# An FFN up projection as seven block products a pair instead of eight, and its FFN in two halves with the activations in DRAM between them

## The chip, the cores and the metric

One NeuronCore of one Trainium2 chip runs the whole program in one launch. The metric is the device time of an execution in microseconds (us), smaller is better. Three timed runs of the kernel before gave 2637.28 to 2642.17 us, median 2638.38.

## The reference

A trunk of two layers over 1024 tokens of width 1024, all float32. Layer 0 mixes tokens with an mLSTM, layer 1 with differential attention. After each mixer comes a LayerNorm, and then the part that matters here, a gated FFN with a causal convolution of width 3 over the tokens:

```
u = x * (1 + sc2) + sh2
h = causal_dwconv(u @ w_up, conv_w, conv_b)     # w_up 1024 x 5632
a, g = split(h, 2)                              # 2816 columns each
y = (gelu(g) * a) @ w_down                      # w_down 2816 x 1024
x = layer_norm(alpha * x + (1 + g2) * y)
```

`sc2`, `sh2` and `g2` come from a conditioning vector through a matrix ("ada").

## The kernel before

Everything is laid out for 128 partitions. To keep float32 accuracy with TensorE's rounded format, each operand is split into a high part (rounded, by ScalarE's cast) and a low part (the rest, by a VectorE subtraction), and each product is three matmuls: high by high, high by low, low by high (`mm3`, L153). A matmul has 128 x 128 weights and 512 columns.

The 2816 hidden columns are 22 pairs: pair i is 128 columns of a and the 128 columns of g that gate them. For each part of a pair `up` (L687) takes one weight unit of 128 x 1024 (eight k tiles of 128), and multiplies it with the transposed normed tokens `uhi`, `ulo` in two halves of 512 tokens: per pair 2 parts x 2 token halves x 8 k tiles x 3 = 96 matmuls, into a PSUM accumulator `big` of two banks, of which there are two. ScalarE applies the last tap and the bias from PSUM (L698), VectorE the two other taps (L700), ScalarE the Gelu (L703), VectorE the product (L704), and both split the result into `ahi`, `alo` (L707, L708), which stay in SBUF.

`down` (L711) multiplies the activations of a group of pairs with their rows of w_down, for eight token tiles and two column halves, into one PSUM bank each (tags a and b, two banks each), and VectorE adds the bank to the residual `z` (L724, L726). `GROUPS` says how many pairs go into a group: 4, 4, 3, 3, 3, 5. After the first pair of a group, the down product of the group before is issued, so that up and down alternate through the FFN.

Weights come through `get` (L117): it issues the DMA of a unit up to four units ahead on SP's queue into one of three `raw` buffers, folds a row vector into it where there is one (`fold_down`, L1035: VectorE multiplies w_down by 1 + g2, L1037), and splits it (L113, L114). `plan` (L986) lists the units in the order of use.

Into an FFN leads `norm_to_u` (L343): per token tile statistics on VectorE and a power on GpSimd (L322), then the normed tile is transposed on TensorE in three groups of tiles (0 to 3, 4 and 5, 6 and 7), scaled and shifted out of PSUM (L300, L302) and split (L303, L304). The residual's own affine by rows (`finish_norm`, L371, L372) is handed out in steps, on VectorE, beside the first pairs. The ada vectors that layer 1 needs are summed on VectorE (L212, L214) between the groups of layer 0's FFN, the last one (for g2 of layer 1) at the entry to layer 1's FFN.

Instructions are traced in program order and put into the engines' queues by a list scheduler that takes, for each engine, what its own timing model holds to be ready, earlier traced first. Tiles of a pool with the same tag share its buffers, and one waits until another is free. `queued` (L132) holds TensorE's instructions in the order of tracing.

## Time and profile before

| | |
|---|---|
| median of three timed runs | 2638.38 us |
| the profiled execution | 2637.58 us |
| its span, first to last instruction | 2635.7 us |
| mean granted TensorE clock | 0.996 |
| busy TensorE, VectorE, ScalarE, GpSimd | 2577.2, 1612.1, 906.6, 56.0 us |
| DMA | 191.97 MB, mean 73 GB/s |

In the profile PE is TensorE's matmul side, PEld its weight loads, DVE VectorE, ACT ScalarE, POOL GpSimd, SP the engine that issues most DMAs. "idle <- X" is the time an engine sat idle before an instruction and what ended it. `out<-in` names the tiles; L126 is the line of `mm`, so matmuls are told apart by tiles: `big<-uhi,whi` is an up product (or a projection of the mLSTM), `bank<-whi,ahi` a down product. The granted clock is 1.00 at 2.4 GHz; the lower of its two levels is 1.2 GHz. Layer 0's FFN runs from about 582 to 1350 us, layer 1's from 1889 to the end.

### The profile page before, as it was taken

How to read it: one execution, taken by the hardware profiler on the slowest of the kernel's cores; microseconds unless marked ns; L12 is line 12 of the kernel's file. 1: busy time of each engine (PE TensorE's matmuls, PEld its weight loads, DVE VectorE, ACT ScalarE, POOL GpSimd, SP SyncE). 2: the span in 40 equal slices, each digit the busy share in tenths (PEclk: the TensorE clock that was granted, in tenths of full speed). 3: DMA queues.
4: the chain of work that ended last, by engine and by line, in shares of the span. 5: the costliest groups of instructions: out<-in, count | busy, mean ns of one | idle time of the engine just before them, and what ended most of it. 6: DMA issues, size and time to landing. Idle time of an engine off the chain costs nothing.

```text
span 2635.7 us, 30418 instructions
## 1 busy us (share of the span) xinstructions
PE 2577.2 (98%) x12380; PEld 2143.3 (81%) x12380; DVE 1612.1 (61%) x2407; ACT 906.6 (34%) x1465; POOL 56.0 (2%) x83
## 2 busy tenths in 40 slices
PE   7999999999999999999999999999999999999998
PEld 5887788877888888888788888878778888888887
DVE  7647546668646466465576777787784444544457
ACT  4423333244212122123246666674432222222120
POOL 0000000000000000000000000000000000000001
PEclk9999999999999999999999999999999999999999
DMA  6415312211313133131131101111221111111102
GB/s 264 144 33 175 96 40 65 85 60 50 103 56 104 56 118 114 48 112 35 56 132 35 35 27 35 35 53 49 102 88 40 56 41 60 52 41 56 48 32 80
DMA packets 59451, 191.97 MB, mean 73 GB/s; under 512 B 6640, under 2 KB 13104, under 8 KB 59312
## 3 DMA queue, kind: packets, MB, share of 16 engines
q1 hardware_dynamic: 56480, 184.30, 20.5%
q10 hardware_dynamic: 2832, 5.74, 0.7%
q8 instruction: 97, 1.59, 0.2%
q14 instruction: 42, 0.34, 0.0%
HBM read 180.04 MB, written 9.98 MB: 72 GB/s over the span
## 4 chain that ended last, share of the span: by engine, by line
PE 86%; DVE 8%; ACT 3%; DMA 1%; issue 1%; POOL 0%; DVEq 0%; ACTq 0%; SPq 0%; POOLq 0%
PE big L126 44%; PE bank L126 40%; PE bank L129 2%; DVE wlo L114 1%; DVE acc L214 1%; ACT whi L113 1%; DMA raw<-in_ada 1%; ACT p L867 1%; DVE qk L466 1%; DVE acc L255 1%; DVE ulo L304 1%; DMA wt<-mscr 0%; DVE col L857 0%; DVE kk L812 0%; DVE z L371 0%
## 5 line engine op out<-in xcount | busy, mean ns | idle before, releaser
L126 PE MATMUL big<-uhi,whi 128*128 128x512 f32 x1664 | 648.5, 391 | 4.2 <-ACT y L698 2.0
L126 PE MATMUL big<-ulo,whi 128*128 128x512 f32 x1664 | 649.7, 390 | 1.8 <-DVE ulo L304 1.6
L126 PE MATMUL big<-uhi,wlo 128*128 128x512 f32 x1664 | 648.1, 389 | 0.0
L113 ACT CAST whi<-raw 128x1024 fp32r<-128x1024 f32 x204 | 211.6, 1052 | 809.9 <-PE big L126 454.3
L114 DVE TENSOR_TENSOR wlo<-raw,whi 128x1024 fp32r<-128x1024 f32 x204 | 247.0, 1222 | 337.9 <-ACT whi L113 331.5
L126 PEld LDWEIGHTS big<-uhi,whi 128*128 128x128 f32 x1664 | 312.2, 188 | 70.5 <-ACT y L698 2.4
L126 PEld LDWEIGHTS big<-ulo,whi 128*128 128x128 f32 x1664 | 312.3, 188 | 68.6 <-DVE ulo L304 4.1
L126 PEld LDWEIGHTS big<-uhi,wlo 128*128 128x128 f32 x1664 | 312.4, 188 | 64.3 <-issue 0.2
L126 PE MATMUL bank<-whi,ahi 128*128 128x512 f32 x704 | 274.7, 390 | 0.0
L126 PE MATMUL bank<-wlo,ahi 128*128 128x512 f32 x704 | 274.7, 390 | 0.0
L126 PE MATMUL bank<-whi,alo 128*128 128x512 f32 x704 | 274.0, 390 | 0.0
L700 DVE SCALAR_TENSOR_TENSOR y<-big,pp,y 128x1023 f32<-128x1023 f32 (+1 forms) x176 | 225.0, 1278 | 2.6 <-ACT y L698 0.4
L726 DVE TENSOR_TENSOR z<-z,bank 128x512 f32<-128x512 f32 x160 | 109.5, 685 | 143.9 <-PE bank L126 143.5
L126 PE MATMUL bank<-whi,hot 128*128 128x512 f32 x512 | 175.1, 404 | 3.6 <-ACT hot L386 2.1
L126 PE MATMUL bank<-whi,uhi 128*128 128x256 f32 (+1 forms) x480 | 171.5, 358 | 2.2 <-ACT v L799 2.0
L126 PE MATMUL bank<-wlo,uhi 128*128 128x256 f32 (+1 forms) x480 | 160.7, 335 | 0.0
L126 PE MATMUL bank<-whi,ulo 128*128 128x256 f32 (+1 forms) x480 | 160.1, 336 | 0.0
L126 PEld LDWEIGHTS bank<-wlo,ahi 128*128 128x128 f32 x704 | 132.1, 188 | 29.8 <-issue 2.2
L126 PEld LDWEIGHTS bank<-whi,ahi 128*128 128x128 f32 x704 | 132.2, 188 | 28.6 <-ACT ahi L707 0.5
L126 PEld LDWEIGHTS bank<-whi,alo 128*128 128x128 f32 x704 | 132.1, 188 | 28.4 <-issue 1.1
L698 ACT ACTIVATE y<-big,pp 128x1024 f32<-128x1024 f32 x88 | 106.1, 1206 | 50.0 <-PE big L126 50.0
L126 PEld LDWEIGHTS bank<-whi,hot 128*128 128x128 f32 x512 | 96.1, 188 | 24.7 <-ACT hot L386 2.9
(226 smaller groups left out, 3512.1 us busy)
## 6 DMA issues: line engine op xcount, KB each, us to landing
raw<-in_up SPq DMA_DIRECT2D x88, 512.0 KB, 3.3
raw<-in_ada SPq DMA_DIRECT2D x80, 512.0 KB, 3.3
raw<-in_dn SPq DMA_DIRECT2D x44, 512.0 KB, 3.3
ada<-in_ada SPq DMA_DIRECT2D x16, 512.0 KB, 8.5
raw<-in_vo SPq DMA_DIRECT2D x16, 512.0 KB, 4.2
raw<-in_qk SPq DMA_DIRECT2D x16, 512.0 KB, 4.3
raw<-in_dqk SPq DMA_DIRECT2D x16, 512.0 KB, 3.3
xt<-in_xT SPq DMA_DIRECT2D x8, 512.0 KB, 9.6
```

The lines of the kernel that those rows point to most:

```text
L113: nc.scalar.copy(hi[:, :n], raw[:, :n])
L114: nc.vector.tensor_sub(lo[:, :n], raw[:, :n], hi[:, :n].bitcast(F32))
L126: self.last = self.nc.tensor.matmul(out, lhsT=lhsT, rhs=rhs, start=start, stop=stop, **kw).ins
L129: self.last = self.nc.tensor.transpose(out, in_, self.idn if idn is None else idn).ins
L214: nc.vector.scalar_tensor_tensor(acc, raw, self.cs[:, k:k + 1], acc, op0=ALU.mult, op1=ALU.add)
L255: last = nc.vector.scalar_tensor_tensor(acc, raw[:, i, :], c, acc, op0=ALU.mult, op1=ALU.add).ins
L304: nc.vector.tensor_sub(lo, tmp, hi.bitcast(F32))
L466: nc.vector.scalar_tensor_tensor(t[:, d:], ps[:, :S - d], wc(3 - d), t[:, d:], op0=ALU.mult, op1=ALU.add)
L698: nc.scalar.activation(y, ps, AF.Identity, bias=self.pp[:, base + 132 + ch:base + 132 + ch + 1], scale=wc(2))
L700: nc.vector.scalar_tensor_tensor(y[:, d:], ps[:, :S - d], wc(2 - d), y[:, d:], op0=ALU.mult, op1=ALU.add)
L726: nc.vector.tensor_add(z, z, ps)
L867: nc.scalar.activation(p[:, :nk], ps_[c][:, :nk], AF.Exp, bias=mx[:, c:c + 1], accum_out=sums[:, c, i:i + 1])
```

## The change

The up products of a pair form a 2 x 2 block product: the parts a and g by the two token halves, over two halves of the contraction (four k tiles each). Strassen's scheme (in Winograd's form) does it with seven block products instead of eight. It needs sums of weight blocks (`sums`, four additions of 128 x 512 on GpSimd per pair), sums of token blocks once at the entry (`ffn_entry`: T1 to T4, on VectorE and GpSimd), and sums of products (`p1` to `p7`, copies on ScalarE, additions on VectorE). One half comes out with its sign turned, so the convolution taps of g are negated at the start. The convolution now reads SBUF tiles `ca` and `cg` instead of PSUM. P3 and P4 of a pair are issued in the turn of the next one.

All 22 pairs go first. Their activations are stored in DRAM (`ascr`), and the down half loads them again and splits them beside the down weights (`prepare`); the fold of 1 + g2 goes to GpSimd. The groups are 3, 4, 4, 4, 4, 3. The normed residual is stored at the entry (`nscr`), loaded before the down half, and its affine is done there on GpSimd. The ada vectors are taken in single steps, in layer 0 all in the down half, in layer 1 in the up loop. The FFN's units leave `plan`, and its second weight pool is gone in layer 1.

The core of the diff:

```diff
-GROUPS = (4, 4, 3, 3, 3, 5)
+GROUPS = (3, 4, 4, 4, 4, 3)
...
+        nc.vector.tensor_scalar(taps, taps, -1.0, None, op0=ALU.mult)
...
+    def product(self, out, w, b, first):
+        (whi, wlo) = w
+        for j, (bhi, blo) in enumerate(b):
+            c = slice(j * P, (j + 1) * P)
+            self.mm3(out, whi[:, c], wlo[:, c], bhi, blo, first and j == 0, j == 3, skip_group_check=True)
+
+    def ffn_entry(self, zs, fp, ln, layer, early):
...
+                if t0 == 0:
+                    B["11" if k < 4 else "21"][k % 4] = parts(dst, self.up, "u", 24)
+            if t0 == 0:
+                early(B)
+        for j in range(4):
+            top, bot = u[j], u[4 + j]
+            nc.vector.tensor_sub(top[:, lo_], top[:, hi_], top[:, lo_])
+            nc.gpsimd.tensor_tensor(top[:, hi_], bot[:, hi_], top[:, hi_], op=ALU.subtract)
+            hi, lo = wide(top, self.up, "u", 24)
+            B["T1"][j], B["T3"][j] = (hi[:, lo_], lo[:, lo_]), (hi[:, hi_], lo[:, hi_])
+            B["22"][j] = parts(bot[:, hi_], self.up, "u", 24)
+            nc.vector.tensor_sub(bot[:, hi_], bot[:, hi_], top[:, lo_])
+            nc.gpsimd.tensor_tensor(bot[:, lo_], bot[:, hi_], bot[:, lo_], op=ALU.subtract)
+            hi, lo = wide(bot, *((self.up, "u", 24) if j < 2 else (fp, "f", 17)))
+            B["T4"][j], B["T2"][j] = (hi[:, lo_], lo[:, lo_]), (hi[:, hi_], lo[:, hi_])
...
+        def sums(i):
+            if i < NPAIR:
+                st1[i], st2[i] = ftile("st1"), ftile("st2")
+                add = lambda o, x, y: nc.gpsimd.tensor_tensor(o, x, y, op=ALU.add)
+                add(st1[i][:, lo_], rg[i][:, lo_], rg[i][:, hi_])
+                add(st1[i][:, hi_], st1[i][:, lo_], ra[i][:, lo_])
+                add(st2[i][:, lo_], ra[i][:, lo_], rg[i][:, lo_])
+                add(st2[i][:, hi_], ra[i][:, hi_], st1[i][:, hi_])
...
+        def p1(i):
+            pa[i] = self.bigbank()
+            with self.queued():
+                self.product(pa[i][:, lo_], cut(wx[i], lo_), B["11"], True)
+            cg[i] = ftile("cg")
+            nc.scalar.copy(cg[i][:, lo_], pa[i][:, lo_])
...
+        def p3(i):
+            with self.queued():
+                self.product(pc[i], w4[i], B["22"], False)
+            nc.vector.tensor_add(ca[i][:, hi_], ca[i][:, hi_], pc[i])
+            return conv(ca[i], i)
+
+        def p4(i, ya):
+            with self.queued():
+                self.product(pa[i][:, hi_], ww[i], B["T4"], False)
+            nc.vector.tensor_add(cg[i][:, lo_], cg[i][:, lo_], pa[i][:, hi_])
+            yg = conv(cg[i], NPAIR + i)
             nc.scalar.activation(yg, yg, AF.Gelu)
             nc.vector.tensor_mul(ya, ya, yg)
...
+            nc.sync.dma_start(out=self.ascr[i], in_=ya)
...
+        for i in range(NPAIR):
+            if i > 1:
+                p1(i)
+            prep_rest(i)
+            load(i + 2, 0)
+            sums(i + 1)
+            p5(i)
+            if i > 1:
+                p2(i)
+            if i:
+                prep_x(i + 1)
+            if i > 1:
+                next(beside_up, None)
+            load(i + 2, 1)
+            p6(i)
+            prep_y(i + 1)
+            if i:
+                ya = p3(i - 1)
+                p4(i - 1, ya)
+            if i == NPAIR - 1:
+                prepare_to(2)
+            p7(i)
+        for tt in range(NT):
+            zs[tt] = utile("z", F32)
+            nc.scalar.dma_start(out=zs[tt], in_=self.nscr[tt * P:(tt + 1) * P, :])
...
+        for tt in range(NT):
+            nc.gpsimd.tensor_tensor(zs[tt], zs[tt], rows[0], op=ALU.mult)
+            nc.gpsimd.tensor_tensor(zs[tt], zs[tt], rows[1], op=ALU.add)
```

## Rows read from the trace of the kernel before

**Rows 1.** The page: each engine's busy time, share of span, instructions.
```profile
PE 2577.2 (98%) x12380; PEld 2143.3 (81%) x12380; DVE 1612.1 (61%) x2407; ACT 906.6 (34%) x1465; POOL 56.0 (2%) x83
```

**Rows 2.** The page: the chain that ended last, by engine.
```profile
PE 86%; DVE 8%; ACT 3%; DMA 1%; issue 1%; POOL 0%; DVEq 0%; ACTq 0%; SPq 0%; POOLq 0%
```

**Rows 3.** Stretches: length, busy time (instructions) by engine, clock, DMA.
```profile
core 0: us, PE busy (x) PEld busy (x) DVE busy (x) ACT busy (x) POOL busy (x), PEclk, DMA share, GB/s
582.30:618.30 36.00, 31.51 (x162) 24.11 (x160) 35.77 (x55) 27.05 (x48) 1.42 (x1) 1.00 0.22 74
...
700.00:1310.00 610.00, 609.53 (x2678) 498.19 (x2677) 330.34 (x359) 138.00 (x130) 2.20 (x4) 1.00 0.23 77
...
1888.60:1931.50 42.90, 38.10 (x189) 29.14 (x188) 40.74 (x65) 29.76 (x50) 1.96 (x2) 1.00 0.50 172
...
2000.00:2565.00 565.00, 565.00 (x2494) 467.83 (x2493) 267.18 (x257) 130.53 (x123) 0.00 (x0) 1.00 0.14 48
```

**Rows 4.** Chain in time, layer 1: start, length, engine, tile, line, matmuls.
```profile
2062.30 87.04 PE big L126 x384
2149.34 43.52 PE bank L126 x192
...
2573.66 54.43 PE bank L126 x240
```

**Rows 5.** VectorE's groups by shape: busy us, mean ns, idle before.
```profile
L114 DVE TENSOR_TENSOR wlo<-raw,whi 128x1024 fp32r<-128x1024 f32 x204 | 247.0, 1222 | 337.9 <-ACT whi L113 331.5 <-PE bank L129 4.8 <-PE bank L126 0.4
L700 DVE SCALAR_TENSOR_TENSOR y<-big,pp,y 128x1022 f32<-128x1022 f32 x88 | 112.6, 1280 | 2.2
...
L726 DVE TENSOR_TENSOR z<-z,bank 128x512 f32<-128x512 f32 x160 | 109.5, 685 | 143.9 <-PE bank L126 143.5
L214 DVE SCALAR_TENSOR_TENSOR acc<-raw,cs,acc 128x1024 f32<-128x1024 f32 x70 | 89.5, 1279 | 15.9 <-DMA raw<-in_ada 15.6
...
L304 DVE TENSOR_TENSOR ulo<-utmp,uhi 128x512 fp32r<-128x512 f32 x24 | 16.3, 685 | 2.8 <-ACT uhi L303 2.8
...
L300 DVE TENSOR_SCALAR utmp<-bank,as,ab 128x256 f32<-128x256 f32 x16 | 8.0, 533 | 0.0
```

**Rows 6.** ScalarE's groups by shape, as above.
```profile
L113 ACT CAST whi<-raw 128x1024 fp32r<-128x1024 f32 x204 | 211.6, 1052 | 809.9 <-PE big L126 454.3 <-PE bank L126 283.1 <-DMA raw<-in_up 32.7
L698 ACT ACTIVATE y<-big,pp 128x1024 f32<-128x1024 f32 x88 | 106.1, 1206 | 50.0 <-PE big L126 50.0
L703 ACT ACTIVATE y<-y 128x1024 f32<-128x1024 f32 x44 | 46.7, 1062 | 125.0 <-DVE y L700 124.9
...
L386 ACT CAST hot<-bank 128x512 fp32r<-128x512 f32 x32 | 18.6, 587 | 40.2 <-PE bank L129 40.2
```

**Rows 7.** Timeline, GpSimd's power and VectorE beside it: start, length, instruction.
```profile
579.09 0.55 POOL L322 TENSOR_TENSOR col<-col,mhalf 128x1 f32<-128x1 f32 x1 [4.91 <-DVE col L321]
...
588.21 1.23 DVE L371 TENSOR_TENSOR z<-z,lng 128x1024 f32<-128x1024 f32 x1
588.42 1.42 POOL L322 TENSOR_TENSOR col<-col,mhalf 128x1 f32<-128x1 f32 x1 [8.79 <-DVE col L321]
589.35 0.68 DVE L304 TENSOR_TENSOR ulo<-utmp,uhi 128x512 fp32r<-128x512 f32 x1
...
1457.55 1.65 POOL L906 TENSOR_TENSOR col<-col,mhalf 128x8 f32<-128x8 f32 x1 [114.90 <-DVE col L905]
```

**Rows 8.** The page's DMA issues: queue, count, KB, median us to landing.
```profile
raw<-in_up SPq DMA_DIRECT2D x88, 512.0 KB, 3.3
```

**Rows 9.** Layer 1's norm: TensorE matmuls in time, and stretches (columns: rows 3).
```profile
1341.22 0.28 PE L126 MATMUL bank<-wlo,uhi 128*128 128x256 f32 x1
...
1352.36 0.41 PE L126 MATMUL bank<-wlo,uhi 128*128 128x256 f32 x1
...
1345.00:1350.00 5.00, 3.79 (x14) 2.11 (x14) 3.48 (x8) 3.96 (x10) 0.00 (x0) 0.61 0.00 0
1350.00:1360.00 10.00, 8.01 (x51) 8.02 (x52) 7.12 (x10) 2.14 (x8) 0.00 (x0) 0.68 0.46 177
```

**Rows 10.** Timeline, VectorE's last z additions, with the idle time before.
```profile
2621.31 0.69 DVE L726 TENSOR_TENSOR z<-z,bank 128x512 f32<-128x512 f32 x1 [1.10 <-PE bank L126]
...
2628.11 0.69 DVE L726 TENSOR_TENSOR z<-z,bank 128x512 f32<-128x512 f32 x1 [1.10 <-PE bank L126]
```

More of the change, by code (lines that the diff above doesn't have):

```diff
@@ L214, in ada_vector @@
                 nc.vector.scalar_tensor_tensor(acc, raw, self.cs[:, k:k + 1], acc, op0=ALU.mult, op1=ALU.add)
-        self.ada_late = (layer, n, acc)
+            if k == KT - 1:
+                self.ada_late = (layer, n, acc)
+            yield
+    def ada_vector(self, layer, n, pool):
+        for _ in self.ada_steps(layer, n, pool):
+            pass
     def finish_ada(self):
@@ new lines, in early @@
+        def early(b):
+            nonlocal B
+            B = b
+            p1(0)
+            p2(0)
+            load(1, 1)
+            prep_x(1)
+            p1(1)
+            p2(1)
+        B = None
+        load(0, 0)
+        load(0, 1)
+        load(1, 0)
+        sums(0)
+        prep_x(0)
+        self.ffn_entry(zs, fp, ln, layer, early)
+        prep_y(0)
+        groups, i = [], 0
+        for g in GROUPS:
+            groups.append(list(range(i, i + g)))
+            i += g
+        act, dn, held = {}, {}, {}
@@ new lines, in ffn, with fetch @@
+        homes = [(ftile,) * 4 + (utile,) * 8] + [(utile, ftile) * 8] * 4 + [(ftile,) * 8 + (wtile,) * 4]
+        work = []
+        for g, members in enumerate(groups):
+            slots = iter(homes[g])
+            for m in members:
+                for kind in range(2):
+                    work.append((g, m, kind, (next(slots), next(slots))))
+        def fetch(x):
+            if x < len(work) and x not in held:
+                g, m, kind, _ = work[x]
+                held[x] = self.raw()
+                nc.sync.dma_start(out=held[x], in_=(self.ascr[m], self.a["dn"][layer, m])[kind])
@@ new lines, in prepare, with prepare_to @@
+        def prepare(x):
+            g, m, kind, slots = work[x]
+            fetch(x)
+            fetch(x + 1)
+            raw = held.pop(x)
+            if kind:
+                nc.gpsimd.tensor_tensor(raw, raw, self.gb[(layer, 1)], op=ALU.mult)
+            hi, lo = (s(n, F32R) for s, n in zip(slots, ("dhi", "dlo")))
+            (act, dn)[kind][m] = hi, lo
+            nc.scalar.copy(hi, raw)
+            nc.vector.tensor_sub(lo, raw, hi.bitcast(F32))
+        done = 0
+        def prepare_to(n):
+            nonlocal done
+            while done < n:
+                prepare(done)
+                done += 1
@@ new lines, in ffn @@
+        for tt in range(NT):
+            zs[tt] = utile("z", F32)
+            nc.scalar.dma_start(out=zs[tt], in_=self.nscr[tt * P:(tt + 1) * P, :])
+        rows = self.ln_rows(self.wa, ln, "w", 8)
+        ya = p3(NPAIR - 1)
+        prepare_to(4)
+        p4(NPAIR - 1, ya)
+        prepare_to(2 * GROUPS[0])
+        for tt in range(NT):
+            nc.gpsimd.tensor_tensor(zs[tt], zs[tt], rows[0], op=ALU.mult)
+            nc.gpsimd.tensor_tensor(zs[tt], zs[tt], rows[1], op=ALU.add)
+        for g, members in enumerate(groups):
+            base = done
+            more = 2 * GROUPS[g + 1] if g + 1 < len(groups) else 0
+            late = after() if after and g + 1 == len(groups) else None
@@ L726, in down @@
                         nc.vector.tensor_add(z, z, ps)
+                    prepare_to(base + min(more, (more * (2 * tt + half + 1) + 13) // 14))
+                    if half:
+                        next(beside_down, None)
                     for _ in range(3):
-                        if after and after[0] <= tt - 1:
-                            after[0] = next(after[1], NT + 9)
-            if after:
-                for _ in after[1]:
-                    pass
-        pending, i, first = None, 0, True
-        for gi, g in enumerate(GROUPS):
-            members = list(range(i, i + g))
-            i += g
-            for n, m in enumerate(members):
-                up(m)
-                for _ in range(min(3, len(steps))):
-                    steps.pop(0)()
-                if n == 0 and pending is not None:
-                    down(pending, first)
-                    first = False
-            pending = members
-            self.finish_ada()
-            if gi < len(fillers):
-                fillers[gi]()
-        down(pending, first, after and after())
+                        if late and late[0] <= tt - 1:
+                            late[0] = next(late[1], NT + 9)
+            if late:
+                for _ in late[1]:
+                    pass
+            elif g + 2 == len(groups):
+                for _ in beside_down:
+                    pass
     def rel_bias(self):
```

198 lines of the change are left out of this document (120 added, 78 removed).

## The prediction

> **What bounds the kernel now.** I read the page's engine row first: TensorE is busy for 98% of the span [rows 1], and the chain that ended last is 86% TensorE and 8% VectorE [rows 2]. A busy share can hide short waits, so I looked at stretches: in the bodies of both FFNs (700 to 1310 us and 2000 to 2565 us) TensorE works 609.5 of 610 and 565.0 of 565 us at full clock, and VectorE 330 and 267 us [rows 3]. There the chain runs in pieces of 384 matmuls in 87.04 us and 192 in 43.52 us, both 0.2267 us a matmul [rows 4]. So the body is bound by the number of matmuls, and a matmul less is 0.2267 us less as long as the others keep up. The two entries to an FFN (582 to 618, 1889 to 1931 us) are different: VectorE is busy 35.8 of 36.0 us and 40.7 of 42.9 us, TensorE 31.5 and 38.1 us [rows 3]. They are bound by VectorE. The sum below is made against the profiled execution, 2637.6 us (span 2635.7 and 1.9 around it), 0.8 below the median of 2638.4.
>
> **What goes.** An up pair has eight block products of 12 matmuls (four k tiles by three terms), 96 x 0.2267 = 21.76 us; afterwards seven, 84 x 0.2267 = 19.04. Over 44 pairs that is 528 matmuls, **-119.7 us**. The down projection keeps its 1056 matmuls a layer.
>
> **The up loop.** Per pair VectorE gets three 512-wide subtractions for w3, w4, ww (0.685 each), one 1024-wide for x (1.222), one scalar_tensor_tensor for y (1.279), five 512-wide additions of products (0.685), four convolution steps (1.28), one product (1.22) [rows 5]: 14.3 us in 15 instructions. Back to back a next one starts 0.09 early (588.21 + 1.23 against 589.35, [rows 7]), so some 13.0 us. ScalarE gets five 512-wide copies (0.587), two 1024-wide (1.052), two biases (1.206) and the Gelu (1.062): 8.5 us [rows 6]. GpSimd gets four 512-wide additions, for which the trace has no row. From below, its shortest instruction is 0.55 us; from above, its power over eight elements took 1.65 against 0.55 for one, 0.16 us an element, which would make 80 us of 512 [rows 7]. That is another function; an addition is nearest to VectorE's row for the same shape, so I take GpSimd's fixed 0.55 and that 0.685, 1.23 us, 4.9 a pair. All three fit under 19.04 us: TensorE should stay the bound on average.
>
> The tight place is an order, not a sum. A pair's last product, P4, is issued one pair late, and the product block P1 of the pair after needs the accumulator that P4 leaves; only P7 (2.72 us) lies between. VectorE's addition that empties it stands behind the other half's convolution: after P3 ends, addition 0.69, ScalarE's bias 1.21, two steps 2.38, together 4.27, which is 1.55 after P4 ends; with its own 0.69 it is done at 2.24 of 2.72. Slack: 0.5 us. And GpSimd's four additions for the next pair fall there: their second operand lands about 3.3 us after its issue [rows 8], which waits for x to be split, some 12 us into the pair, so they start near 15.5 of 19, when those convolution steps begin. Do the engines disturb one another? GpSimd's one-element power takes 0.55 us, but 1.42 where it started 0.21 us into a VectorE operation on two SBUF tensors, and it ended when that had [rows 7]. So GpSimd waits for VectorE; whether VectorE waits for a long GpSimd operation no row shows. The Trainium skill, in "SBUF — State Buffer", section "SBUF: two separate sides", says that the two share one pair of ports and that the first to start holds it for its whole instruction, the other blocked; the 1.42 us row agrees with that for one side. By that rule two waits of up to 1.23 eat the 0.5 us and cost 2.0 us a pair, which is a rival below. I take 0.4 us a pair over some 42 pairs, **+17** (0 to +84).
>
> **The entries.** The change takes VectorE's z affine and, in layer 1, eight ada steps of 1.28 out of the entry, and the splitting of some weights. It adds, for each of four j, three 512-wide and two 1024-wide operations (3 x 0.685 + 2 x 1.22 = 4.5 us, 4.1 back to back [rows 5]), 16.4 in all, with eight GpSimd subtractions beside. VectorE's list then: two x splits 2.3, eight block splits 4.9, eight 256-wide affines 3.6 (0.53 each, less the overlap), last tile's addition and statistics 2.5, blocks 16.4, y 1.2: 31 us. Full rate can begin near 33 us after the last mixer matmul, where before it was 36 and 42.9. But before then TensorE had 96 matmuls done, and now 48 early ones and perhaps 10 of P5 and P6, the rest needing the last j: 38 x 0.2267 = 8.6 us behind. So +5.6 in layer 0 and -1.3 in layer 1. To that come the latencies of five engine changes in the last j, some 3 us each layer, and the clock: in the norm ahead of the attention, after waits and sparse transposes, the granted clock of two stretches was 0.61 and 0.68, between the 2.4 and the 1.2 GHz level, and 256-wide matmuls took 0.41 instead of 0.28 us [rows 9]; I take 2 us a layer. Together +14; with GpSimd's subtractions (8 x 1.23 = 9.8 a layer) in VectorE's way for 3 of that in each **+20** (+6 to +34).
>
> **The turn from up to down.** Before, the last pairs' activations were ready long before use, since up and down alternated. Now the down half begins 5.4 us (P3, P4) after the last P7. In that time VectorE has to end two pairs (about 10.5 us from these rows) and split operands of members 1 and 2 of the first group (four times 1.22 less the overlap, 4.5) and P7's sums (1.2): some 16 us. Four banks of PSUM let TensorE start members that are there, up to 5.4 us more. 16 - 10.8 leaves 5 to 6 us a layer. Then z: its affine, 16 VectorE passes a layer before, moves to GpSimd, with 22 folds of the down weights (on VectorE any two-tensor operation of 1024 takes 1.22 [rows 5]). At 0.55 + 1.22 = 1.77, sixteen passes and seven folds until the first group ends are 41 us, and from z's reload (its buffers come free with the last P2, 16 us before the down half, less 3.3 for the DMA [rows 8]) to the group's end (144 matmuls, 32.6 us) there are 46 us. It just fits; I add 3 us a layer. **+18** (+4 to +50). "GPSIMD Engine Reference", section "Elementwise — side-by-side cycle accounting", in the Trainium skill, gives 4497 ns for 2048 elements of such an addition; by an estimate from it a pass is 2.2 us and the 41 become 51, 5 us late a layer, no row here shows it.
>
> **The tails.** In layer 1's last group VectorE waits 1.10 us in each period of 6.80 [rows 10]: 5.7 us of work for a token tile that TensorE takes 6.80 for (five members, 54.43 us in all [rows 4]). With three members TensorE takes 4.08, VectorE still 5.7: the last group lasts 2 + 8 x 5.7 + 2 = 50 us where 32.6 + the old 7.6 us after the last matmul would be 40. **+9.** In layer 0 the norm of the next layer has the same group beside it; its VectorE work nearly equals TensorE's, **+4** (both 5 to 22 together).
>
> **At nothing:** 44 activation stores and reloads and the z rows each way, 63 MB in all. A pair's three transfers of 512 KB in 19 us are 83 GB/s; the body moved 77 GB/s at a DMA share of 0.23 [rows 3]. The store waits on SP for the pair's last product with the next loads behind it; these are wanted a pair later. If raw's three buffers fail to cover that, the wait is 3.3 us for some pairs. The ada vectors of layer 1 go into the down half (40 x 1.28 = 51 us of VectorE in 239), the sign of the gate taps is one small operation at the start, 0.5 us.
>
> Sum: -119.7 + 17 + 20 + 18 + 13 + 0.5 = -51; 2637.6 - 51 = **2586 us**, own range 2556 to 2615.
>
> **Rivals.**
> A. GpSimd and VectorE block each other, and P4's accumulator comes free late: 2.0 us x 42 = 84, entries at 34, turn at 38, tails 13: +49, 2687 us. From (119.7 - 52) / 42 = 1.6 us a pair it ends slower than before. For it: the 1.42 us row and the timing above. Against: VectorE kept its 0.68 us right beside GpSimd at 589.35 [rows 7], and if that addition goes ahead of the convolution steps, nothing is late.
> B. Nearly all is covered: up loop 0, entries +8, turn +6, tails +10: -96, 2542 us. For it: every engine's sum is under 19.04. Against: entries and tails are VectorE-bound already.
> C. The up loop holds, but z's passes and folds on GpSimd come late and the down half waits with full banks, 15 us a layer instead of 3: 2610 us.
>
> **Chances.** Forecast 0.52, A 0.18, B 0.17, C 0.13. A ends faster than before in a sixth of its part. Differences under 0.2% (5 us) can't be told here: faster 0.80, same 0.05, slower 0.15. Range 2542 to 2645: it takes in C and most of B, and A up to 1.7 us a pair.
>
> **What would show it.** Each steady pair: 84 matmuls in 19.0 to 19.8 us; over 20.6 is rival A, and the wait before P1 then names VectorE's addition. GpSimd's additions at 1.2 us, or longer where VectorE runs. After the last mixer matmul a TensorE gap of about 10 us at the entry, one of 5 to 9 at the turn, VectorE without waits in the last group. Wrong altogether if a steady matmul takes more than 0.227, or if the loop waits for a load.

## The result

The changed kernel takes 2778.23 us (median of 4 runs, 2776.4 to 2782.76) where the kernel before took 2640.2 beside it: 1.0526 times as long (95% interval 1.0508 to 1.0545), 5% slower. The forecast was 2586, in a range of 2542 to 2645: wrong in sign and size. The figures from here to the experiments are from a profiled execution with a span of 2776.6 us, 140.9 more than before. By stage (the first instruction of one to the first of the next) that is +6.3 in the mLSTM, +77.3 in layer 0's FFN (847.0 against 769.7), +0.6 in the attention and +56.7 in layer 1's FFN (803.8 against 747.1).

The page of the kernel after: engines, and the chain that ended last (answering to [rows 1, 2]).

```profile
PE 2523.6 (91%) x11852; PEld 2063.0 (74%) x11852; DVE 1931.9 (70%) x2692; ACT 1045.5 (38%) x1675; POOL 593.4 (21%) x351
...
PE 74%; DVE 10%; ACT 5%; POOL 4%; DMA 4%; issue 3%; DVEq 0%; POOLq 0%; ACTq 0%; SPq 0%
```

The 528 matmuls are gone (12380 to 11852), but TensorE fell from 98% busy to 91%. Its waits, summed over the execution (waiting tile and line, releaser: us, times, longest):

```profile
PE bank L126 <- ACT dhi L892: 54.6, 7, 13.4
PE big L126 <- ACT ca L802: 53.5, 39, 1.9
PE bank L126 <- DVE dlo L893: 26.0, 4, 12.4
PE bank L126 <- ACT uhi L711: 24.8, 6, 4.6
```

Three kinds of place: many short ones (ca: 39 of them, one in nearly every pair), a few long ones for a down operand (dhi, dlo: the turns), and the entries (uhi). Stretches of the kernel after (columns as in [rows 3]): layer 0's up loop, its turn, layer 1's entry:

```profile
640.00:1070.00 430.00, 398.76 (x1709) 318.83 (x1709) 328.48 (x310) 173.76 (x206) 147.68 (x85) 0.99 0.23 79
1077.00:1135.00 58.00, 19.26 (x65) 14.03 (x63) 35.52 (x18) 10.67 (x11) 53.34 (x19) 0.67 0.23 81
1967.00:2035.00 68.00, 45.11 (x190) 31.81 (x189) 50.33 (x65) 36.62 (x54) 21.54 (x15) 0.80 0.11 42
```

Before, TensorE was idle for 0.5 us of the 1175 us that [rows 3] shows of the two bodies. Now it idles 7% of the loop and two thirds of the turn, where GpSimd is busy 53 of 58 us. On top of these waits the granted clock of the turn is 0.67, between the two levels.

One pair of the up loop, in layer 0: GpSimd first, then VectorE, ScalarE and TensorE (start, length, instruction).

```profile
825.23 3.22 POOL L765 TENSOR_TENSOR st<-raw 128x512 f32<-128x512 f32 x2 [13.76 <-DMA raw<-in_up]
828.41 1.74 POOL L765 TENSOR_TENSOR st<-st,raw 128x512 f32<-128x512 f32 x1
830.22 2.15 POOL L765 TENSOR_TENSOR st<-raw,st 128x512 f32<-128x512 f32 x1
```

```profile
827.31 1.68 DVE L786 TENSOR_TENSOR w<-st,w 128x512 fp32r<-128x512 f32 x1
828.92 2.31 DVE L826 SCALAR_TENSOR_TENSOR y<-ca,pp,y 128x1023 f32<-128x1023 f32 x1
831.15 0.67 DVE L838 TENSOR_TENSOR cg<-cg,big 128x512 f32<-128x512 f32 x1
831.75 1.70 DVE L826 SCALAR_TENSOR_TENSOR y<-ca,pp,y 128x1022 f32<-128x1022 f32 x1
833.37 0.68 DVE L786 TENSOR_TENSOR ww<-raw,ww 128x512 fp32r<-128x512 f32 x1
833.98 1.27 DVE L826 SCALAR_TENSOR_TENSOR y<-cg,pp,y 128x1023 f32<-128x1023 f32 x1
```

```profile
840.15 1.04 ACT L774 CAST xhi<-raw 128x1024 fp32r<-128x1024 f32 x1 [1.95 <-PE big L126]
841.10 0.58 ACT L802 COPY ca<-big 128x512 f32<-128x512 f32 x1
```

```profile
841.73 0.50 PE L126 MATMUL big<-uhi,yhi 128*128 128x512 f32 x1 [1.39 <-ACT ca L802]
```

Beside GpSimd a split of 128x512 takes 1.68 instead of 0.68 and a convolution step 2.31 and 1.70 instead of 1.27; an addition with one operand in PSUM (L838) keeps its 0.67. GpSimd's additions take 1.6 to 2.2; one that had no VectorE operation beside it, at 593.51 us, took 1.27. What TensorE waits for in this pair is none of that: P6 starts when ScalarE has copied P2's result, and that copy stands behind the cast of the next pair's weights.

The turn of layer 0 on GpSimd, on VectorE (one split of those beside the passes) and on TensorE (waits in brackets):

```profile
1081.66 13.01 POOL L934 TENSOR_TENSOR z<-z,lng 128x1024 f32<-128x1024 f32 x4 [23.28 <-DMA lng<-in_lng]
1094.63 12.29 POOL L935 TENSOR_TENSOR z<-z,lnb 128x1024 f32<-128x1024 f32 x4
1106.88 4.63 POOL L934 TENSOR_TENSOR z<-z,lng 128x1024 f32<-128x1024 f32 x2
1111.47 2.34 POOL L889 TENSOR_TENSOR raw<-raw,gb 128x1024 f32<-128x1024 f32 x1
1113.77 5.67 POOL L935 TENSOR_TENSOR z<-z,lnb 128x1024 f32<-128x1024 f32 x2
```

```profile
1085.83 3.36 DVE L893 TENSOR_TENSOR dlo<-raw,dhi 128x1024 fp32r<-128x1024 f32 x1
```

```profile
1095.81 0.79 PE L126 MATMUL bank<-dlo,dhi 128*128 128x512 f32 x1 [10.59 <-DVE dlo L893]
1114.94 0.79 PE L126 MATMUL bank<-dhi 128*128 128x512 f32 x1 [11.10 <-ACT dhi L892]
...
1135.03 1.22 PE L126 MATMUL bank<-dhi 128*128 128x512 f32 x2 [13.39 <-ACT dhi L892]
```

The passes over z come in fours of 13.0 and 12.3 us, 3.1 to 3.3 us each. The fold of a down weight (L889), which TensorE's next operand needs, stands behind ten of them. And the split of a down operand on VectorE, 1.22 us long where it is undisturbed, takes 3.36 beside a pass.

### The profile page after: what moved, and what is told of

The parts are those of the page before. It is cut to its first block, busy times and chain, and to the rows that moved or that the text cites. A ratio compares the mean times of both kernels' runs of the same rounds, so it can differ in the third digit from the quotient of the medians.

```text
span 2776.6 us, 30737 instructions
## 1 busy us (share of the span) xinstructions
PE 2523.6 (91%) x11852; PEld 2063.0 (74%) x11852; DVE 1931.9 (70%) x2692; ACT 1045.5 (38%) x1675; POOL 593.4 (21%) x351
## 4 chain that ended last, share of the span: by engine, by line
PE 74%; DVE 10%; ACT 5%; POOL 4%; DMA 4%; issue 3%; DVEq 0%; POOLq 0%; ACTq 0%; SPq 0%
PE bank L126 43%; PE big L126 29%; PE bank L129 2%; DMA raw<-in_ada 2%; ACT xhi L774 1%; POOL z L935 1%; POOL z L934 1%; DVE wlo L114 1%; DVE acc L216 1%; DMA raw<-in_dn 1%; ACT ca L802 1%; DMA wt<-mscr 1%; DVE dlo L893 1%; DVE acc L263 1%; ACT p L1084 1%
## 5 line engine op out<-in xcount | busy, mean ns | idle before, releaser
L126 PE MATMUL bank<-dhi 128*128 128x512 f32 x704 | 281.2, 401 | 56.8 <-ACT dhi L892 54.6
L126 PE MATMUL bank<-dlo,dhi 128*128 128x512 f32 x704 | 281.6, 400 | 26.0 <-DVE dlo L893 26.0
L126 PE MATMUL bank<-dhi,dlo 128*128 128x512 f32 x704 | 280.6, 399 | 0.0
L765 POOL TENSOR_TENSOR st<-raw 128x512 f32<-128x512 f32 x88 | 143.7, 1653 | 507.1 <-DMA raw<-in_up 469.6
L126 PE MATMUL big<-ub,xhi 128*128 128x512 f32 x704 | 223.0, 397 | 4.7 <-DVE ub L705 4.4
L893 DVE TENSOR_TENSOR dlo<-raw,dhi 128x1024 fp32r<-128x1024 f32 x88 | 138.5, 1580 | 72.7 <-ACT dhi L892 72.4
L126 PEld LDWEIGHTS bank<-dlo,dhi 128*128 128x128 f32 x704 | 136.1, 193 | 58.2 <-DVE dlo L893 28.1
L889 POOL TENSOR_TENSOR raw<-raw,gb 128x1024 f32<-128x1024 f32 x44 | 108.9, 2476 | 308.2 <-DMA raw<-in_dn 259.9
L826 DVE SCALAR_TENSOR_TENSOR y<-ca,pp,y 128x1023 f32<-128x1023 f32 x88 | 169.3, 1923 | 6.9 <-ACT y L824 6.8
L126 PEld LDWEIGHTS bank<-dhi,dlo 128*128 128x128 f32 x704 | 136.3, 194 | 28.9 <-issue 0.5
L126 PE MATMUL big<-ub,xlo 128*128 128x512 f32 x352 | 137.3, 390 | 0.0
```

What stands on the lines that cost most here:

```text
L126: self.last = self.nc.tensor.matmul(out, lhsT=lhsT, rhs=rhs, start=start, stop=stop, **kw).ins
L765: add = lambda o, x, y: nc.gpsimd.tensor_tensor(o, x, y, op=ALU.add)
L826: nc.vector.scalar_tensor_tensor(y[:, d:], src[:, :S - d], wc(2 - d), y[:, d:], op0=ALU.mult, op1=ALU.add)
L889: nc.gpsimd.tensor_tensor(raw, raw, self.gb[(layer, 1)], op=ALU.mult)
L893: nc.vector.tensor_sub(lo, raw, hi.bitcast(F32))
```

## Experiments

Each kernel was run beside the kernel before on the same chip. "So many us less" is the difference of two such ratios times 2640 us; the intervals of the ratios, about 0.002 to either side, make it good to some 6 us. L numbers are those of the changed kernel.

### One suspect at a time

**The passes over z on VectorE.**

```diff
-            nc.gpsimd.tensor_tensor(zs[tt], zs[tt], rows[0], op=ALU.mult)
-            nc.gpsimd.tensor_tensor(zs[tt], zs[tt], rows[1], op=ALU.add)
+            nc.vector.tensor_tensor(...)   # both
```

> The residual's affine at the turn (16 passes a layer, 3.0 us each on GpSimd) is done by VectorE. Theory 1 (GpSimd's queue: the folds of the down weights stand behind these passes, and TensorE waits for folded weights): TensorE's gaps at layer 0's turn, 38.8 us in 1077 to 1135 us, fall below 15 us, and the time by about 50 us over both layers, to 2725 us. Rival (the reloaded activations and down weights come late from DRAM through three buffers): the gaps stay and the time changes by less than 10 us. Rival (VectorE is the full engine at the turn, and takes 18 us more now): slower by up to 15 us a layer.

2747.11 us, ratio 1.0409 (1.0393 to 1.0424): 31 us less than the changed kernel. The waits for dhi fell from 54.6 to 9.1 us, but 31.1 us of waits for z itself took their place, one of 15.8 at each turn: the sixteen passes now stand ahead of the first additions in VectorE's queue.

**The folds on VectorE.**

```diff
-                nc.gpsimd.tensor_tensor(raw, raw, self.gb[(layer, 1)], op=ALU.mult)
+                nc.vector.tensor_tensor(raw, raw, self.gb[(layer, 1)], op=ALU.mult)
```

> The fold of the down weights is done by VectorE, the residual's affine stays on GpSimd. Theory 1 (the folds stand behind the affine on GpSimd): the folded weights come early, TensorE's gaps at the turn fall to 15 us a layer, what is left being VectorE's additions to a residual that is late; about 40 us less, 2738 us. Rival (the affine itself gates the first group, through additions that wait and PSUM banks that stay full): the gain is below 15 us. Rival (loads): no change.

2761.82 us, 1.0466 (1.0448 to 1.0483): 16 less, where the theory said 40. Two gaps of 10 us stay at layer 0's turn. VectorE is busy 54.8 of its 58 us, and beside the passes over z its splits and folds take 3.4 us each instead of 1.22.

**Product three ahead of product six.**

```diff
-            p6(i)
-            prep_y(i + 1)
             if i:
                 ya = p3(i - 1)
+            p6(i)
+            prep_y(i + 1)
+            if i:
                 p4(i - 1, ya)
```

> P3 of the pair before is issued between P2 and P6, so that ScalarE's copy of P2 has 2.7 us before P6, which waits for it 1.4 us in each of 39 pairs now. Theory 2 (this order costs the 1.4 us): a steady pair goes from 20.9 to 19.2 or 19.4 us, 60 to 65 us less in all, 2715 us. Rival (GpSimd and VectorE blocking each other set the pair; the wait only shows where it comes out): the wait moves to another product, the pair stays above 20.5 us, less than 15 us gained.

2748.49 us, 1.0412 (1.0396 to 1.0427): 30 less, half of what the theory said. The period fell from 20.91 us (15 of L838 from 705.6 to 998.4) to 19.95, not to 19.04. The wait for ca is gone; TensorE now waits 19.1 us, 32 times, for L838, which frees P4's accumulator. That is rival A's place. VectorE's and GpSimd's forms in this run, 700 to 1050 us (busy, mean ns):

```profile
L781 DVE SCALAR_TENSOR_TENSOR ylo<-st,yhi 128x1024 fp32r<-128x1024 f32 x18 | 40.4, 2245 | 0.0
L826 DVE SCALAR_TENSOR_TENSOR y<-ca,pp,y 128x1022 f32<-128x1022 f32 x18 | 32.1, 1785 | 0.0
...
L786 DVE TENSOR_TENSOR ww<-raw,ww 128x512 fp32r<-128x512 f32 x18 | 30.9, 1715 | 0.0
...
L765 POOL TENSOR_TENSOR st<-raw 128x512 f32<-128x512 f32 x34 | 66.6, 1978 | 205.9 <-DMA raw<-in_up 205.9
```

**The condition rows of layer 0 in buffers of their own.**

```diff
-            raw = self.raw()
+            raw = self.rada.tile([P, D], F32, tag="f", ...) if self.rada else self.raw()
```

> In layer 0's down half the ada rows go through one buffer of their own and no longer through the three buffers of the reloads and down weights. Theory 3 (three buffers for three streams: in 1135 to 1235 us, behind the turn, TensorE issues only some 85 us of matmuls in 100): this stretch runs at full rate, 15 us less, and a little less still in the turn: 2760 us. Rival (the stretch is a consequence of the late turn alone, the groups after it being behind in their preparation): less than 5 us.

2768.3 us, 1.0487 (1.0471 to 1.0502): 10 less, of 15 expected. Between 1135 and 1235 us TensorE is busy 95.3 instead of 89.5 us.

### The up loop: order, engine, lock

**Product three ahead, and the sums on VectorE.**

```diff
-                add = lambda o, x, y: nc.gpsimd.tensor_tensor(o, x, y, op=ALU.add)
+                add = lambda o, x, y: nc.vector.tensor_tensor(o, x, y, op=ALU.add)
```

> The up loop with product three ahead of product six (the order of the run that took 2748.5 us) and, besides, the four additions of a pair's weights on VectorE instead of GpSimd. Theory (GpSimd and VectorE hold each other up in operations that read two tensors): no VectorE operation of the up loop stands beside a GpSimd sum any more, the two-tensor ones come back from 1.7 to 2.3 us to 1.28 us, the wait of TensorE for the addition that frees product four's accumulator (19.1 us over 32) goes below 5 us, the pair's period falls from 19.9 to about 19.2 us, and the time to about 2720 us. Rival (VectorE's queue is simply too full in the up loop): the four additions bring it 2.7 us a pair more, the wait for the accumulator stays or grows, and the time is 2745 to 2780 us.

2711.13 us, 1.0254 (1.0236 to 1.0272): 72 less than the changed kernel, 42 less than with the order alone. The period in layer 0 is 19.04 us (15 of L838 from 715.7 to 982.3), 84 matmuls back to back; in layer 1, where the ada vectors are taken beside the loop, it is 19.50. With more work VectorE is faster (700 to 1050 us):

```profile
L826 DVE SCALAR_TENSOR_TENSOR y<-ca,pp,y 128x1023 f32<-128x1023 f32 x18 | 23.1, 1283 | 26.2 <-ACT y L824 26.2
...
L781 DVE SCALAR_TENSOR_TENSOR ylo<-st,yhi 128x1024 fp32r<-128x1024 f32 x17 | 20.7, 1218 | 0.0
...
L786 DVE TENSOR_TENSOR ww<-raw,ww 128x512 fp32r<-128x512 f32 x17 | 11.7, 686 | 0.0
```

**The sums on VectorE, in the old order.** The same line alone.

> The after kernel with the sums on VectorE and nothing else: product six stays ahead of product three. Theory (in the after kernel's order the bound is product six's wait for ScalarE's copy of product two, which stands behind the cast of the next pair's weights; the lock only decides once that wait is gone): the 53.5 us of that wait stay within 10 us, and the time is 2755 to 2778 us. Rival (the lock is the whole loss of the up loop, and the order had a part only through it): about 2715 to 2735 us.

2761.02 us, 1.0444 (1.0425 to 1.0463), as the theory said. The wait for ca stays at 52.9 us. Order alone gives 30 us, engine alone 22, both 72. The traces of the two loops alone show it more sharply. What they take beyond their matmuls is 77 us in the changed kernel, 47 with the order, 71 with the engine and 16 with both; so most of the 22 came elsewhere. Each fix hides the other, as the loop has two late places and a pair is as late as the later one.

**Additions on GpSimd that nobody wants**, in the kernel with order and sums mended:

```diff
             prep_rest(i)
+            for _ in range(4):
+                nc.gpsimd.tensor_tensor(st2[i][:, lo_], B["11"][0][0].bitcast(F32), B["21"][0][0].bitcast(F32), op=ALU.add)
```

> The kernel with product three ahead and the sums on VectorE (2711.1 us), and beside it four additions of 128x512 a pair on GpSimd whose operands lie ready, whose result nobody reads and for which nothing waits but the buffer's next owner. Theory (the two engines hold each other up while both read two tensors): VectorE's two-tensor operations of the up loop grow again, from 1.28 us towards 1.5 to 2.3 us, TensorE waits again for the addition that frees product four's accumulator, and the time rises by 15 to 40 us, to 2726 to 2751 us, although no result of GpSimd is wanted. Rival (the sums were simply late on GpSimd, and moving them made them early): additions that nobody waits for cost nothing, 2708 to 2714 us.

2814.64 us, 1.0648 (1.0627 to 1.0669): 104 us more than without them, more than twice the top of what the theory expected. The theory had the place wrong too: TensorE's new wait is for P6's addition (L812, 82.4 us over 40), not for L838 (4.2 us). 700 to 1050 us:

```profile
L775 DVE TENSOR_TENSOR xlo<-raw,xhi 128x1024 fp32r<-128x1024 f32 x16 | 36.9, 2309 | 0.0
L765 DVE TENSOR_TENSOR st<-st,raw 128x512 f32<-128x512 f32 x16 | 28.5, 1779 | 0.0
L765 DVE TENSOR_TENSOR st<-raw,st 128x512 f32<-128x512 f32 x16 | 28.4, 1775 | 0.0
...
L908 POOL TENSOR_TENSOR st<-ub 128x512 f32<-128x512 f32 x65 | 116.5, 1793 | 240.9 <-DVE w L786 223.1 <-issue 14.0
```

No instruction waits for these additions, and yet three sums on VectorE take 1.78 instead of 0.69 us and the split of x 2.31 instead of 1.22, each 1.09 more; the period is 21.31 us. 4 x 1.09 = 4.4 us a pair; the period grew by 2.3, so 2.1 had been slack. So it is the engines' hold on each other that costs, not the lateness of the sums. Its size seems to depend on whether it falls on operations with slack behind them, which was not foreseen and is not shown further.

### The turn and the entry

**The passes over z on VectorE, a token tile at a time.**

```diff
-        for tt in range(NT):
-            (two passes on GpSimd)
+        z_rows(0)                      # two passes on VectorE
...
                         nc.vector.scalar_tensor_tensor(z, z, ALPHA, ps, op0=ALU.mult, op1=ALU.add)
+                        if half:
+                            z_rows(tt + 1)
```

> Only the turn of the after kernel changed: the two passes that give the first norm's rows to z stand on VectorE, and one token tile at a time, tile t+1 behind the additions of tile t in the first group, instead of all sixteen passes on GpSimd ahead of everything. Theory (the turns lost their time to the order of queues, sixteen passes ahead of the folds of the next group's weights and of the first additions): of the gaps of 10 to 13 us at each turn one of about 10 us is left (the start of the group), and the time is about 2715 us, some 30 us under that with the passes on VectorE but all ahead (2747 us). Rival (the turn is bound by when z and the rows land from DRAM, 23 us behind their issue): the same gap is left as with all passes ahead, 2740 to 2750 us.

2738.21 us, 1.0358 (1.0338 to 1.0378): 44 less than the changed kernel, and only 13 less than with all passes ahead, not 30. The 10 to 13 us gaps of layer 0's turn are gone; the longest left is 3.76 us. The theory's place was right and its size too large: the waits are now short ones, among them ten for z's additions, 21.8 us in all over both layers (3.5 the longest).

**The entry without GpSimd, operands of the fifth product first.**

```diff
-            nc.gpsimd.tensor_tensor(top[:, hi_], bot[:, hi_], top[:, hi_], op=ALU.subtract)
+            nc.vector.tensor_tensor(top[:, hi_], bot[:, hi_], top[:, hi_], op=ALU.subtract)
             (top's casts)
+        for j in range(4):
             (bot's; its second subtraction on VectorE too)
```

> Only the entry of the after kernel changed: its eight GpSimd subtractions a layer stand on VectorE, and the four operands that the fifth product needs are all made before the operands of the sixth, seventh and fourth. Theory (the strict order over four columns, each a chain VectorE, GpSimd, ScalarE, VectorE of about 6 us, starves TensorE): the entry of each layer gets 8 to 12 us shorter and the time is about 2758 us. Rival (VectorE's own work, 24 us in the entry, is the bound and not the chain): less than 4 us a layer, 2770 to 2778 us.

2781.24 us, 1.0518 (1.0498 to 1.0539): nothing gained. The rival holds here. VectorE at the end of this entry:

```profile
630.21 2.33 DVE L712 TENSOR_TENSOR ulo<-ur,uhi 128x1024 fp32r<-128x1024 f32 x1 [1.11 <-ACT uhi L711]
632.46 2.36 DVE L705 TENSOR_TENSOR ub<-ur,ub 128x512 fp32r<-128x512 f32 x2
...
637.73 4.00 DVE L712 TENSOR_TENSOR ulo<-ur,uhi 128x1024 fp32r<-128x1024 f32 x2 [0.51 <-ACT uhi L711]
641.66 3.43 DVE L788 TENSOR_TENSOR w<-st,w 128x512 fp32r<-128x512 f32 x2
```

The subtractions moved, but GpSimd's sums for the next pair still lay beside these splits (2.33 instead of 1.22).

### The two parts of the change

**Two halves, plain products.** All of the Strassen part taken out, the rest kept:

```diff
-        (weight sums, block differences, seven products and their additions)
+        for half in range(2):                                   # eight block products a pair
+            self.proj_cols(ps[:, half * HALF:(half + 1) * HALF], wq[x], half)
+        ya = conv(ps, ...)                                      # from PSUM, as before the change
```

> The two-half structure of the after kernel (activations and z through DRAM, down products in six groups behind the last pair) with the eight plain block products a pair, the entry and the convolution from the accumulators as in the kernel before: no weight sums, no block differences, no separate combination of products. Theory (the two parts of the change cost and gain separately; the halves cost the two turns, about 39 us and 50 us of which most is lost, the later raw buffers and the tails, some 110 to 150 us in all, and the seven products give back only 0 to 40 us of their 119.7): 2755 to 2800 us. Rival (the halves are nearly free and it is Strassen's own work that costs the time): 2650 to 2700 us.

2699.97 us, 1.0207 (1.0187 to 1.0227): far from the theory and just inside the rival's range, though the halves aren't nearly free. The halves cost 2.07%, some 55 us, and the seven products, which should give 119.7 back, cost another 3.19% (5.26 less 2.07), some 84 us, in this structure. The up loop is full again (430.00 of 430 us at 640 to 1070) and a single long gap is left at each turn, here layer 0's:

```profile
1087.22 0.79 PE L126 MATMUL bank<-dhi 128*128 128x512 f32 x1 [14.93 <-ACT dhi L814]
1089.54 0.80 PE L126 MATMUL bank<-dlo,dhi 128*128 128x512 f32 x1 [1.53 <-DVE dlo L815]
```

The passes over z are the same sixteen on GpSimd, but begin 39 us sooner (1042.4 against 1081.7), although the down products begin only 13 us sooner. The reload of z finds free buffers: it is issued at 601 to 620 us, not at 1063 to 1072, where the load of the norm's rows stands behind it. The first four passes take 9.46 us, not 13.01. And the convolution, which reads PSUM here, keeps its time beside them (two steps, beside the passes from 1051.8 on):

```profile
1051.13 2.60 DVE L769 SCALAR_TENSOR_TENSOR y<-big,pp,y 128x1023 f32<-128x1023 f32 x2 [8.13 <-ACT y L767]
```

### Together

**Three fixes:** order, sums and z's passes by token tile, and the condition rows' own buffers, entry as in the change.

> Product three ahead of product six, the weights' sums on VectorE, z's rows on VectorE one token tile at a time, and the condition rows of layer 0's down stage in buffers of their own; the entry stays as in the after kernel. Theory (the loss is a sum of separate waits: up loop 67 us, turns 40 us, raw buffers 10 us): the gains add up to 117 us and the time is about 2661 us. Rival (VectorE, now with the sums and the z passes, takes the place of the waits removed): less than two thirds of it adds up, 2700 us or more.

2667.96 us, 1.0107 (1.0092 to 1.0122): 111 us less than the changed kernel, of 117 expected.

**The entry too:** its subtractions on VectorE, and

```diff
+        for j in range(4):          # last, after T1, T3, T4, T2
+            B["22"][j] = parts(u[4 + j][:, hi_], self.up, "u", 24)
```

> As the run with the three fixes, and the entry of each layer without GpSimd: differences on VectorE, those of the fifth product first, those of the sixth next, and the four splits of the plain block (wanted by the third product, a pair later) last. Theory (the entry is bound by VectorE's own 24 us; of these the plain block's splits, 2.8 us, go behind and the waits for GpSimd go): 4 to 8 us a layer less than the three fixes alone, about 2650 us. Rival (the entry is bound by what PE has in store, four products, whatever the order): within 3 us of the three fixes.

2651.44 us, 1.0042 (1.0027 to 1.0057): 17 less, about what was expected (8 to 16), where much the same step without the sums on VectorE had given nothing. First waits of TensorE in layer 0's entry: 3.27, 0.50, 0.37, 0.46, 0.31 us instead of 4.39, 1.19, 4.55, 0.65, 3.47.

**The folds too**, on VectorE.

> As the run with the entry too, and the folds of the down weights on VectorE instead of GpSimd, so that GpSimd has only the norms left in the FFN. Theory (wherever the two engines meet they prolong each other; at the turn and beside the down products the folds still meet dlo and z passes): 5 to 15 us less than the run with the entry too. Rival (VectorE is full at the turn, and 22 folds of 1.28 us a layer in its queue cost what the lock cost): no change or up to 10 us more.

2634.47 us, 0.9971 (0.9960 to 0.9982): 19 less again, of 5 to 15 expected, and 0.3% ahead of the kernel before. VectorE has more to do, and yet the first 65 us of the two turns hold 17 us less of what isn't matmuls at full rate.

**The order of the condition rows' loads**, beside the entry run:

```diff
-            self.dma_last = nc.sync.dma_start(out=raw, in_=self.a["ada"][layer, n, k]).ins
+            nc.sync.dma_start(out=raw, in_=self.a["ada"][layer, n, k])
```

> As the run with the entry too, but the loads of the condition rows no longer become the transfer that later steps are ordered behind, as in the kernel before. Theory (the 6.3 us that the mLSTM stage lost come from that order: the later steps now wait for the last of these loads): about 6 us less than the run with the entry too, all of it ahead of 582 us of the span. Rival (the loss comes from the shorter look-ahead of weights in that stage): no change.

2654.66 us, 1.0050 (1.0035 to 1.0065): no change. Why the mLSTM stage is about 6 us longer stays open; the shorter look-ahead of weights wasn't tried. In the traces of all these versions the stage ends 1.3 to 7.6 us later than before.

**No condition rows in layer 0's first down group**, on top of all five:

```diff
                     if half:
-                        next(beside_down, None)
+                        for _ in range((0, 2, 2)[g] if g < 3 else 1):
+                            next(beside_down, None)
```

> The kernel with all five fixes (2634.5 us) with the condition rows of the next layer left out of layer 0's first down group and done two a token tile in the second and third. Theory (what is left at the turn is VectorE's queue: z passes, splits, folds and these multiply-adds ahead of the first additions, 20 us of waits for z): the wait of layer 0's turn falls by 4 to 8 us and the time is 2627 to 2631 us. Rival (layer 0's turn is bound by the splits of the next group alone, as layer 1's, which has no such rows): no change, 2633 to 2636 us.

2621.76 us, 0.9914 (0.9892 to 0.9936): 15 less than with the rows there, twice what was expected, and the best of all. The turn itself gave what the theory said: of its first 65 us 18.5 aren't matmuls at full rate, where the run before had 24.7. Another 8 came from layer 0's tail, which nobody had expected: from the last down matmul to layer 1's last mixer matmul it is 557.9 us, where the run before had 566.0 and the kernel before the change 557.6. The norm of the next layer starts earlier there (the first of its eight powers 31.7 us ahead of the last down matmul, not 15.8); why is not shown. Its page:

```profile
PE 2499.3 (95%) x11852; PEld 2061.6 (79%) x11852; DVE 1949.5 (74%) x2960; ACT 1040.4 (40%) x1675; POOL 55.4 (2%) x83
```

GpSimd has the norms' powers left and nothing else. The waits for z are 16.5 us (20.0 in the run before, 31.5 in the entry run).

## Why the prediction was wrong

Its mechanism for the gain was right: 528 matmuls at 0.2267 us, and the mended loop runs in layer 0 at exactly the 19.04 us a pair that [rows 4] gave. What failed is the price of the terms that it set against the gain: 68.5 us, where they came to some 260. The run with plain products puts 55 of these to the halves and 204 (84 + 119.7) to the scheme, but the two are not independent: its turns, counted as in the table, cost 44 us, those of the changed kernel 87. What the trace after gives for each term (length of a stretch less 0.2267 for each up and down matmul that begins in it; the trace has all 2904 of a layer):

| step | predicted | measured | from |
|---|---|---|---|
| matmuls | -119.7 | -119.7 | 528 x 0.2267 |
| up loop | +17 | +77 | first pair's P7 to first down matmul: 433.7 and 432.5 us, 1740 matmuls in each |
| entries | +20 | +54 | last mixer matmul to the end of that P7: 61.7 and 60.8 us for 84; before, to the full rate, 35.9 and 37.6 for 96 |
| turns | +18 | +87 | first 65 us from the first down matmul: 93 and 96 |
| tails | +13 | +17 | last down matmul to next stage: 24.7 against 16.5; to the end: 16.3 against 7.8 |
| behind the turn | 0 | +18 | from there to the last down matmul, layer 0: 261.7 us, 987 matmuls, less the 20.8 that the body before had beside its own; layer 1: 0.8 |
| mLSTM, attention, start | +0.5 | +7 | stage lengths |

These add up to +140, the trace has +140.9.

**The up loop.** "TensorE should stay the bound on average" rested on sums that do hold (with order and sums mended the loop is full, with more work on VectorE). "The tight place is an order" looked at one place, P4's accumulator, and missed another: P6 waits for ScalarE's copy of P2's result, in a queue that I had only summed (8.5 of 19.04 us). At 1.87 us a pair the cost is near that of rival A, 2.0, and by its bound of 1.6 the kernel had to end slower (with rival A's own 85 us for the rest the bound is (119.7 - 85) / 42 = 0.8). But in the kernel as changed rival A's own wait isn't there. It appeared when the other was removed.

**"Whether VectorE waits for a long GpSimd operation no row shows."** It does, in the loop, at the entries and at the turns, and this is the step that priced most of the rest too low: of all fixes those that took work off GpSimd gave the most (sums 42 us behind the order, passes over z 31 to 44, folds 19 on top). I gave it 0.18. "Against: VectorE kept its 0.68 us right beside GpSimd" was a weak row: GpSimd's operation there had one element a partition, the change's have 512. (Nor did that operation end with VectorE's at 589.44 us, but 0.40 later.) The Trainium skill, "SBUF — State Buffer", section "SBUF: two separate sides", names the conditions: a VectorE operation with two SBUF inputs against a GpSimd operation that reads SBUF, whichever starts first holding the port. This trace agrees: 2.31 for two SBUF operands, 0.67 for the addition with one in PSUM, beside the same GpSimd sums. So does the run with unwanted additions: a product that started at 814.31 us, 0.10 before GpSimd's, kept its 1.23, and GpSimd's took 2.28. The change also moved the convolution's input from PSUM to SBUF, and so into reach of GpSimd; I had carried over its 1.28 from a row that read PSUM [rows 5], which holds beside GpSimd only there (1.30 a step in the run with plain products, 1.7 to 3.4 here).

**The turns.** The price of a pass, 1.77 us, was worked out from VectorE's row; undisturbed GpSimd takes 2.34, and the passes took 3.0 on average. The Trainium skill's figure ("GPSIMD Engine Reference", section "Elementwise — side-by-side cycle accounting"), by an estimate 2.2 us a pass, agrees with the undisturbed row. But the price was not all. The passes were counted against the first group's end, as if each token tile's would be ready in its turn, and the folds were added to them as a sum (41 us of 46, which are 45.3 by its own terms). In GpSimd's queue all sixteen passes stand ahead of most folds, and the first waits 23.3 us for its rows' load. Rival C had the late passes and folds, and 15 us a layer for them, where the stretches of the table lost 44 and 43. But TensorE waits there for split operands (dhi, dlo), not with full banks as rival C said.

**The entries.** "Some 3 us each layer" for changes of engine was too little: four columns, each a chain VectorE, GpSimd, ScalarE, VectorE of some 6 us, in strict order. The prediction had also read layer 1's old entry as 42.9 us, from a stretch that begins 5.3 us ahead of the last mixer matmul; from there it is 37.6, and its -1.3 should have been +4. The clock was put at 2 us a layer, at the entries alone. Matmuls that follow one another at 0.43 us instead of 0.23 cost 5.4 and 5.8 us at the entries and 6.3 and 6.6 at the turns (granted clock 0.66 to 0.78). And in layer 0 GpSimd's sums for the first pair stand ahead of the norm's power:

```profile
593.51 1.27 POOL L765 TENSOR_TENSOR st<-raw,st 128x512 f32<-128x512 f32 x1
594.74 0.55 POOL L330 TENSOR_TENSOR col<-col,mhalf 128x1 f32<-128x1 f32 x1
```

VectorE waits 3.74 us for that power and TensorE 3.45 for the blocks behind it; the queue into which the sums were moved hadn't been walked through.

**At nothing.** "The wait is 3.3 us for some pairs" looked at the up half, where raw's buffers do keep up; in the down half of layer 0 they serve activations, weights and condition rows at once. Buffers of their own for the rows gave 10 of these 18 us back; the rest is not explained.

**The tails** were right in layer 1: VectorE is busy for 43.3 of the last 49.6 us, and the end comes 16.3 us after the last matmul, 8.5 more than before, against 9. Layer 0 lost 8 instead of 4, and none of it in the best version.

Rival B (all covered, 2542) was never near: the best version is at 2622. What plain products would take with the same fixes at the turns was not run, so how much of that the seven products give stays open.

## What to carry to other kernels

Before moving elementwise work to GpSimd, list for the same stretch which VectorE operations read two SBUF tensors: each that starts while GpSimd is at an addition grows by about what that addition still has to run, whether or not anybody waits for its result, and filling VectorE further can be the faster way. When a scheme multiplies the small steps between products, walk each engine's queue through one period in order and write down, for every product, which copy or addition it starts on; sums per engine say only that a solution exists. And price a structural cut (here the two halves, 55 us) as a kernel of its own, before what it is for.

## What the hardware showed that was not expected

What an operation on VectorE loses can be told in advance. In the trace of the changed kernel 184 operations that read two SBUF tensors start at least 0.3 us before the end of a running GpSimd operation of 512 or 1024 columns. All of them grew, each by what GpSimd's operation still had to run, less 0.10 to 0.23 us: VectorE's runs behind it, not beside it. 113 operations of 512 columns with an operand in PSUM, started in the same way, took their 0.67 to 0.69 us.

In the run with additions that nobody wants 217 of 227 grew by the same rule; the other ten kept their time, and GpSimd's additions took 4.0 to 4.6 us there. In its steady pairs the growth is always the same 1.09 us, at 512 (0.69 to 1.78) and at 1024 columns (1.22 to 2.31), since each of the four starts 1.23 us before the end of one of GpSimd's: the two engines take turns, an instruction each. Beside a 1024-wide pass over z it was 2.14 (1.22 to 3.36, at 1085.83 us). GpSimd loses too: its four took 7.38 us instead of 5.1.
